# One Trainium2 core, a blocked fp16 matmul with per-row scales: each row tile's output factor is made on ScalarE in place of GpSimd, and the written-out orders are replaced

## The chip, the core and the metric

One core of a Trainium2 chip runs the whole program. The metric is the time of one execution on the device in microseconds (us). Engines are named as the profile names them: PE is TensorE (matmuls), DVE is VectorE, ACT is ScalarE, POOL is GpSimd, SP is SyncE, which issues all DMAs of this kernel. A "step" in this text is four matmuls of 128x128 by 128x512.

## What is computed

```python
def reference(x, w):                      # x: (8, 2048, 2048) f32, w: (2048, 2048) f32
    cs = np.cumsum(x, axis=1)
    diff = cs - np.concatenate([zeros, cs[:, :-1, :]], axis=1)
    return np.matmul(diff, w).astype(np.float32)
```

The difference of a running sum is x again, so the kernel computes x @ w: 16,384 rows (128 row tiles of 128 rows) by 2048 columns.

## The kernel before

**Stages.** The first four row tiles (PLAIN = 4) are multiplied plainly in bf16 while w streams in from HBM: steps `plain.h.r.ko` (column half h, row tile r, block ko of the inner dimension; two matmuls, one for h = 0 and r = 3). Ahead of them stand 30 `warm` matmuls on zeros and eight groups `turn x.q.a` of eight transposes, which turn the first rows on PE (`cast x` on DVE makes them bf16, `turned x` copies them out of PSUM). Each w block is loaded (`w.h.ko`, 512 KB), cast to bf16 on ACT (`cast w`) and searched for its largest magnitude on DVE (`max w`). From those maxima come `uw` and `uinv`, the factors that put w into fp16.

The remaining 124 row tiles go through groups of four, one group to a "period" (period 0 is `group_plain`, periods 1 to 30 are `group`). A group takes the row tiles g, h = g+2, g+1 and h+1, so its 512 rows by 2048 columns are a 2x2 block product done with seven block products in place of eight, and most of those seven are themselves done in seven quarter products. `P1` to `P5` are such inner seven (class `Quarters`, steps `P1.0` to `P1.6`); `S2g T2`, `S2h T2`, `S3g T3`, `S3h T3` are block products in four steps each. DVE makes the sums and differences of the operands: `S1g`, `S3h` and so on (128x1024), `P5.s1` to `P5.s4` (128x512), `in5.Q3` and others (128x2048), and adds results to results in SBUF (`C11g+P2.g.1`, `add_one`, L576) and in PSUM (`P1.middle`, `P1.last`, L517). ACT copies partial sums out of PSUM (`P1.first`, `P1.out2`, `P1.out4`, L568) and takes scaled results out (`keep C11g.0`, `keep_one`, L565).

**The chain of a row tile** (rows of the next group are prepared during this one; the number in a label is the row tile's place, 4 and 6 being the next g and h, 5 and 7 the next g+1 and h+1). `load4.0`, `load4.1`: two halves of a tile into one of four staging slots F, 512 KB each. `weigh4.0`, `weigh4.1` (ACT, L138): sums of magnitudes of each row. `mean4` (DVE, L157), `scale4` (DVE, L159): the row's scale and its reciprocal. `unit4` (L160): the row's mean times `uw`, a 128x1 value, the factor that every result of that row tile is multiplied with, on ACT in `keep` and on DVE in `add`. `narrow4.0`, `narrow4.1` (ACT, L170): the rows times the reciprocal, to fp16. `turn4.0`, `turn4.1` (DMA transposes). In the group's steady order `unit4` is not read before the next group's `keep C11g.0`.

**What sets the order.** `record` collects every operation with a label and an engine; `emit` sorts them by the table `places` (a number for each label and period; the key None holds the order of periods 3 to 28, while 0, 1, 2, 29, 30 and 31 have their own) and issues them so. Each engine runs its operations in that order, one queue for each engine; waits between engines are semaphores that follow from the order. The 512-wide accumulators are eight PSUM banks, and a bank, a staging slot, a half of the operand room of `P5` (`P5.s3` reuses that of `P5.s1`, `P5.s4` that of `P5.s2`) or the buffer `flow` (which `in1.Q4`, `in5.Q3`, `in3.Q1` and others fill in turn) is overwritten only when its readers are done.

Of the kernel before, what the change touches and what calls it, by code (L numbers as in the profile page):

```python
# [10 lines left out]
def kernel(  # L11
# [108 lines left out]
    def role(t):  # L120
        return t - PLAIN - 4 * period[0]
# [26 lines left out]
    def scale_of(t):  # L148
        if t < END:
            m2 = sums_of.pop(t)  # L150
            m = means_at[t % 4]
            s = scales[t] = scales_at[t % 8]
            u = unit[t] = units_at[t % 8]
            record(
                f"mean{role(t)}",
                "dve",
                lambda: nc.vector.tensor_scalar(m, m2[:, :1], m2[:, 1:], TINY, ADD, MAX),  # L157
            )
            record(f"scale{role(t)}", "dve", lambda: nc.vector.reciprocal(s, m))  # L159
            record(f"unit{role(t)}", "pool", lambda: nc.gpsimd.tensor_scalar(u, m, uw, None, MUL))  # L160
# [967 lines left out]
    for g in range(PLAIN + 4, END, 4):  # L1128
# [8 lines left out]
            'first x.0.2': 0, 'first x.1.1': 1, 'first x.0.0': 2, 'first x.1.3': 3,  # L1137
            'first x.0.3': 4, 'first x.0.1': 5, 'first x.1.2': 6, 'first x.1.0': 7, 'w.0.0': 8,
            'zeros': 9, 'ones': 10, 'numbers': 11, 'numbers turned': 12, 'eye': 13, 'eye#2': 14,
            'eye#3': 15, 'eye#4': 16, 'cast x.0.1': 17, 'cast w.0.0': 18, 'warm.0': 19,  # L1140
            'warm.1': 20, 'warm.2': 21, 'warm.3': 22, 'warm.4': 23, 'warm.5': 24, 'warm.6': 25,
            'warm.7': 26, 'warm.8': 27, 'warm.9': 28, 'warm.10': 29, 'warm.11': 30, 'warm.12': 31,
            'warm.13': 32, 'warm.14': 33, 'warm.15': 34, 'warm.16': 35, 'warm.17': 36,
            'warm.18': 37, 'warm.19': 38, 'warm.20': 39, 'warm.21': 40, 'turn x.0.1': 41,
            'warm.22': 43, 'warm.23': 44, 'warm.24': 45, 'warm.25': 46, 'warm.26': 47,
            'warm.27': 48, 'warm.28': 49, 'turned x.0.1': 50, 'cast x.1.0': 51, 'cast x.0.0': 52,
            'turn x.1.0': 53, 'turned x.1.0': 54, 'cast x.1.1': 55, 'warm.29': 56, 'turn x.0.0': 57,
            'turned x.0.0': 58, 'plain.0.1.0': 59, 'plain.0.0.0': 60, 'w.0.1': 61,
            'plain.0.3.0': 62, 'cast w.0.1': 63, 'plain.0.3.1': 64, 'plain.0.2.0': 65,
            'first x.2.3': 66, 'plain.0.0.1': 67, 'w.0.2': 68, 'plain.0.1.1': 69, 'cast w.0.2': 70,  # L1150
            'plain.0.1.2': 71, 'plain.0.0.2': 72, 'plain.0.2.1': 73, 'turn x.1.1': 74, 'w.0.3': 75,
            'cast w.0.3': 76, 'plain.0.0.3': 77, 'w.0.4': 78, 'cast w.0.4': 79, 'plain.0.1.3': 80,
            'plain.0.2.2': 81, 'plain.0.1.4': 82, 'turned x.1.1': 83, 'plain.0.0.4': 85,
            'max w.0.0': 86, 'max w.0.4': 87, 'w.0.5': 88, 'cast w.0.5': 89, 'plain.0.2.3': 90,
            'plain.0.0.5': 91, 'plain.0.1.5': 92, 'plain.0.3.2': 93, 'plain.0.2.4': 94,
            'plain.0.2.5': 95, 'plain.0.3.3': 96, 'plain.0.3.4': 97, 'first x.2.1': 98,
            'first x.2.2': 99, 'first x.2.0': 100, 'w.0.6': 101, 'cast w.0.6': 102, 'w.0.8': 103,
            'w.0.7': 104, 'first x.3.1': 105, 'w.0.9': 106, 'w.0.10': 107, 'cast x.2.0': 108,
            'turn x.2.0': 109, 'turned x.2.0': 110, 'cast x.2.1': 111, 'max w.0.5': 112,
            'max w.0.3': 113, 'max w.0.8': 114, 'max w.0.1': 115, 'max w.0.2': 116,  # L1160
            'max w.0.7': 117, 'first x.3.0': 118, 'cast x.3.0': 119, 'max w.0.10': 120,
            'max w.0.6': 121, 'first x.3.2': 122, 'first x.3.3': 123, 'w.0.11': 124,
            'cast x.3.1': 125, 'cast w.0.7': 127, 'plain.0.0.6': 128, 'plain.0.3.5': 129,
            'plain.0.1.6': 130, 'cast w.0.8': 131, 'plain.0.2.6': 132, 'turn x.2.1': 133,
            'plain.0.3.6': 134, 'plain.0.0.7': 135, 'plain.0.1.7': 136, 'plain.0.1.8': 137,
            'turned x.2.1': 139, 'plain.0.2.7': 140, 'plain.0.0.8': 141, 'plain.0.3.7': 142,
            'plain.0.2.8': 143, 'cast w.0.9': 144, 'plain.0.1.9': 145, 'plain.0.0.9': 146,
            'cast w.0.10': 147, 'turn x.3.0': 148, 'turned x.3.0': 149, 'cast w.0.11': 150,
            'w.0.12': 152, 'w.0.13': 153, 'w.0.14': 154, 'w.0.15': 155, 'w.1.1': 156, 'w.1.0': 157,
            'max w.0.12': 158, 'max w.0.13': 159, 'max w.0.14': 160, 'max w.0.9': 161,  # L1170
            'max w.0.11': 162, 'max w.1.1': 163, 'max w.0.15': 165, 'plain.0.3.8': 166,
            'plain.0.3.9': 167, 'plain.0.0.10': 168, 'plain.0.2.9': 169, 'plain.0.1.10': 170,
            'plain.0.2.10': 171, 'plain.0.3.10': 172, 'plain.0.3.11': 173, 'turn x.3.1': 174,
            'cast w.0.12': 175, 'turned x.3.1': 176, 'cast w.0.13': 178, 'plain.0.0.11': 179,
            'plain.0.1.11': 180, 'plain.0.0.12': 181, 'plain.0.2.11': 182, 'plain.0.1.12': 183,
            'plain.0.2.12': 184, 'cast w.0.14': 185, 'cast w.0.15': 186, 'w.1.7': 187, 'w.1.2': 188,
            'max w.1.7': 190, 'max w.1.0': 191, 'max w.1.2': 192, 'w.1.3': 193, 'w.1.5': 194,
            'max w.1.5': 195, 'w.1.4': 196, 'w.1.6': 197, 'w.1.9': 198, 'w.1.8': 199, 'w.1.11': 200,
            'w.1.12': 201, 'w.1.13': 202, 'max w.1.3': 203, 'max w.1.6': 204, 'max w.1.4': 205,
            'max w.1.9': 206, 'max w.1.8': 207, 'max w.1.11': 210, 'max w.1.12': 211,  # L1180
            'max w.1.13': 212, 'cast w.1.1': 213, 'plain.0.3.12': 214, 'plain.0.3.13': 215,
            'plain.0.1.13': 216, 'plain.0.0.13': 217, 'plain.0.2.13': 218, 'plain.0.3.14': 219,
            'plain.0.1.14': 220, 'plain.0.3.15': 221, 'plain.0.2.14': 222, 'plain.0.1.15': 223,
            'plain.0.2.15': 224, 'plain.0.0.14': 225, 'plain.0.0.15': 226, 'out.0.3.0': 228,
            'cast w.1.0': 229, 'plain.1.3.0': 230, 'plain.1.3.1': 231, 'out.0.1.1': 232,
            'out.0.1.0': 233, 'plain.1.1.0': 234, 'plain.1.1.1': 235, 'out.0.2.1': 236,
            'out.0.2.0': 237, 'cast w.1.2': 238, 'out.0.0.0': 240, 'out.0.0.1': 241,
            'cast w.1.3': 242, 'plain.1.2.0': 243, 'plain.1.2.1': 244, 'plain.1.1.2': 245,
            'plain.1.2.2': 246, 'cast w.1.4': 249, 'cast w.1.5': 251, 'plain.1.0.0': 252,
            'plain.1.0.1': 253, 'plain.1.3.2': 254, 'cast w.1.7': 255, 'cast w.1.6': 256,  # L1190
            'plain.1.0.2': 257, 'plain.1.0.3': 258, 'plain.1.1.3': 259, 'cast w.1.8': 260,
            'cast w.1.9': 262, 'plain.1.0.4': 263, 'plain.1.3.3': 264, 'plain.1.1.4': 265,
            'plain.1.2.3': 266, 'plain.1.1.5': 267, 'plain.1.3.4': 268, 'plain.1.3.5': 269,
            'plain.1.0.5': 270, 'plain.1.2.4': 271, 'plain.1.2.5': 272, 'plain.1.2.6': 273,
            'plain.1.3.6': 274, 'plain.1.2.7': 276, 'plain.1.2.8': 277, 'plain.1.0.6': 278,
            'cast w.1.12': 280, 'cast w.1.11': 281, 'w.1.10': 282, 'cast w.1.10': 284,
            'w.1.14': 285, 'w.1.15': 286, 'plain.1.3.7': 288, 'plain.1.3.8': 289,
            'plain.1.0.7': 290, 'plain.1.0.8': 292, 'plain.1.1.6': 293, 'plain.1.1.7': 294,
            'cast w.1.13': 295, 'plain.1.1.8': 296, 'cast w.1.14': 297, 'plain.1.3.9': 298,
            'plain.1.1.9': 300, 'plain.1.0.9': 301, 'plain.1.0.10': 302, 'cast w.1.15': 304,  # L1200
            'plain.1.0.11': 305, 'plain.1.0.12': 306, 'plain.1.0.13': 308, 'plain.1.1.10': 309,
            'plain.1.0.14': 310, 'plain.1.1.11': 312, 'plain.1.2.9': 314, 'plain.1.0.15': 316,
            'plain.1.3.10': 320, 'plain.1.3.11': 321, 'put out.0.1.1': 324, 'load0.0': 325,
# [244 lines left out]
            'C21g+P4.g.0': 2158, 'put1.0.0': 2163,  # L1448
        },
        31: {  # L1450
            'P4.last': 455, 'C21h+P4.h.1': 456, 'put-1.0.1': 496, 'C21h+P4.h.0': 567,
            'put-1.0.0': 1083,
        },
        None: {
# [75 lines left out]
```

## Time and profile before

| | |
|---|---|
| time before, median of 3 runs | 1452.06 us (1451.21 to 1452.2) |
| the profiled execution: its time, its span | 1451.33 us, 1449.5 us |
| PE busy | 1440.0 us (99%), 6706 matmuls |
| DVE busy | 1339.7 us (92%) |
| ACT busy | 1129.8 us (78%) |
| POOL busy | 43.3 us (3%) |
| granted TensorE clock | 1.00 |
| DMA, HBM | mean 243 GB/s over the span; 90% busy in a steady group |

The span runs from the first to the last instruction of the trace; the time of the same execution is 1.83 us longer. A wait is put down to the engine whose semaphore came last. Matmuls are pipelined: four in a row are drawn 1.03 us long, and the next four start 0.86 us after them.

### The profile page before, as it was taken

The numbers are of one execution on the slowest core, as the hardware profiler recorded it, in microseconds if no ns is written. First come the engines' busy times: TensorE is split into PE (matmuls) and PEld (weight loads), VectorE is DVE, ScalarE is ACT, GpSimd is POOL, SyncE is SP. The second block draws the span as 40 slices with busy tenths as digits, with TensorE's granted clock in tenths as the row PEclk, the third lists the DMA queues.
The fourth block names the chain that finished last, engine by engine and source line by source line (L and its number), as shares of the span: only waits on it lengthen the run. The fifth ranks groups of instructions, "written<-read, shape, count | busy, mean of one in ns | idle before, by whom it ended". The sixth has DMA issues, their size and how long they took to land.

```text
span 1449.5 us, 20480 instructions
## 1 busy us (share of the span) xinstructions
PE 1440.0 (99%) x6706; PEld 653.6 (45%) x6706; DVE 1339.7 (92%) x2457; ACT 1129.8 (78%) x1742; POOL 43.3 (3%) x129
## 2 busy tenths in 40 slices
PE   8999999999999999999999999999999999999998
PEld 4444444444444444444444444444444444444443
DVE  6998899999999999999999999999999999999998
ACT  5987678887778877778877788877788777788773
POOL 0000000000000000000000000000000000000000
PEclk9999999999999999999999999999999999999999
DMA  9999978999888899988898888998889988888973
GB/s 362 375 263 263 245 200 235 237 252 252 232 222 240 238 263 238 235 220 236 242 273 224 227 233 239 252 249 229 227 238 237 265 243 230 216 242 241 273 204 111
DMA packets 343788, 351.60 MB, mean 243 GB/s; under 512 B 270976, under 2 KB 270976, under 8 KB 343680
## 3 DMA queue, kind: packets, MB, share of 16 engines
q1 hardware_dynamic: 343680, 350.29, 88.5%
q8 instruction: 52, 0.85, 0.2%
q14 instruction: 56, 0.46, 0.1%
HBM read 150.99 MB, written 134.22 MB: 197 GB/s over the span
## 4 chain that ended last, share of the span: by engine, by line
PE 98%; DMA 2%; DVE 0%; ACT 0%; SPq 0%; issue 0%; DVEq 0%; ACTq 0%
PE b L551 61%; PE b L529 33%; PE b L302 3%; DMA W<-in_w_dram 1%; DMA W<-in_x_dram 0%; PE b L430 0%; DVE arena L576 0%; SPq L245 0%; ACT arena L287 0%; PE b L260 0%; DVE b L517 0%; ACT arena L565 0%; DVEq L1525 0%; ACTq L287 0%
## 5 line engine op out<-in xcount | busy, mean ns | idle before, releaser
L529 PE MATMUL b<-W,x 128*128 128x512 f16 x2176 | 532.5, 379 | 0.0
L576 DVE SCALAR_TENSOR_TENSOR arena<-b,tiny,arena 128x512 f32<-128x512 f32 x612 | 447.3, 745 | 12.8 <-PE b L529 2.9
L551 PE MATMUL b<-W,arena 128*128 128x512 f16 x1640 | 410.1, 379 | 0.0
L551 PEld LDWEIGHTS <-arena 128*128 128x128 f16 x2700 | 264.1, 98 | 318.6 <-DVE arena L517 0.2
L565 ACT ACTIVATE arena<-b,tiny 128x512 f32<-128x512 f32 x496 | 327.2, 687 | 54.6 <-PE b L529 29.5
L170 ACT ACTIVATE F<-F,tiny 128x1024 f16<-128x1024 f32 x246 | 282.6, 1149 | 61.9 <-DVE tiny L159 58.1
L529 PEld LDWEIGHTS <-x 128*128 128x128 f16 x2176 | 212.9, 98 | 256.7
L551 PE MATMUL b<-W,x 128*128 128x512 f16 x1180 | 289.0, 379 | 0.0
L138 ACT ACTIVATE waste<-F 128x1024 uint8<-128x1024 f32 x246 | 259.5, 1055 | 5.1 <-DMA F<-in_x_dram 3.2
L551 PE MATMUL b<-arena 128*128 128x512 f16 x1060 | 262.7, 379 | 0.0
L568 ACT COPY arena<-b 128x512 f32<-128x512 f32 x294 | 169.7, 577 | 89.4 <-PE b L551 66.4
L517 DVE TENSOR_TENSOR b<-b,arena 128x512 f32<-128x512 f32 x294 | 202.8, 691 | 31.6 <-ACT arena L565 29.6
L551 PEld LDWEIGHTS <-x 128*128 128x128 f16 x1416 | 138.6, 98 | 167.1
L517 DVE TENSOR_TENSOR arena<-W 128x2048 f16<-128x2048 f16 (+1 forms) x155 | 182.0, 1175 | 4.6 <-PE b L551 4.5
L568 ACT COPY b<-b 128x512 f32<-128x512 f32 x147 | 83.9, 571 | 85.1 <-PE b L551 61.6
L517 DVE TENSOR_TENSOR arena<-W,arena 128x512 f16<-128x512 f16 (+1 forms) x157 | 87.8, 563 | 6.7 <-PE b L551 6.6
L517 DVE TENSOR_TENSOR arena<-x,x 128x1024 f16<-128x1024 f16 (+1 forms) x180 | 89.1, 507 | 1.3 <-PE b L551 1.3
L517 DVE TENSOR_TENSOR x<-x,x 128x1024 f16<-128x1024 f16 x124 | 84.7, 684 | 1.0
L160 POOL TENSOR_SCALAR tiny<-tiny 128x1 f32<-128x1 f32 x124 | 42.7, 352 | 1303.2 <-DVE tiny L157 1295.3
L517 DVE TENSOR_TENSOR arena<-arena 128x512 f16<-128x512 f16 x116 | 49.2, 425 | 17.4 <-PE b L551 11.6
L551 PE MATMUL b<-arena,x 128*128 128x512 f16 x236 | 60.2, 379 | 0.0
L302 PE MATMUL b<-arena 128*128 128x512 bf16 x240 | 53.6, 379 | 2.3 <-ACT arena L287 1.4
(44 smaller groups left out, 513.9 us busy)
## 6 DMA issues: line engine op xcount, KB each, us to landing
F<-in_x_dram SPq DMA_DIRECT2D x246, 512.0 KB, 5.9
out_dram<-arena SPq DMA_DIRECT2D x240, 512.0 KB, 4.4
W<-in_w_dram SPq DMA_DIRECT2D x32, 512.0 KB, 9.6
out_dram<-arena SPq DMA_DIRECT2D x32, 256.0 KB, 3.2
W<-in_x_dram SPq DMA_DIRECT2D x16, 256.0 KB, 6.3
x<-F SPq DMA_TRANSPOSE x246, 4.6
arena<-in_x_dram SPq DMA_DIRECT2D x2, 512.0 KB, 5.3
x<-arena SPq DMA_TRANSPOSE x2, 5.4
```

What stands on the lines that cost most here:

```text
L138: lambda: nc.scalar.activation(waste, data, ABS, scale=1.0 / ROW, accum_out=m),
L160: record(f"unit{role(t)}", "pool", lambda: nc.gpsimd.tensor_scalar(u, m, uw, None, MUL))
L170: lambda: nc.scalar.activation(to, data, COPY, scale=s),
L302: said = nc.tensor.matmul(to[n], xP[:, r, ko, :], b[:, ds(n * NB, NB)], start=(ko == 0), stop=(ko == KO - 1),)
L517: record(label, "dve", lambda: nc.vector.tensor_tensor(dst, p, q, op))
L529: said = nc.tensor.matmul(to[n], a[k], b[k][:, n, :], start=(start and k == 0), stop=(k == KH - 1), skip_group_check=True,)
L551: said = nc.tensor.matmul(to, a[k], b[k], start=(start and k == 0), stop=(k == 3), skip_group_check=True)
L565: record(label, "act", lambda: nc.scalar.activation(c, p, COPY, scale=u))
L568: record(label, "act", lambda: nc.scalar.copy(to, p))
L576: label, "dve", lambda: nc.vector.scalar_tensor_tensor(c, p, u, c, MUL, ADD)
```

## The change

```diff
             record(f"scale{role(t)}", "dve", lambda: nc.vector.reciprocal(s, m))
-            record(f"unit{role(t)}", "pool", lambda: nc.gpsimd.tensor_scalar(u, m, uw, None, MUL))
+            record(
+                f"unit{role(t)}",
+                "act",
+                lambda: nc.scalar.activation(u, m, COPY, scale=uw),
+            )
...
     places = {
         0: {
-            'first x.0.2': 0, 'first x.1.1': 1, 'first x.0.0': 2, 'first x.1.3': 3,
+            'first x.0.3': 0, 'first x.0.2': 1, 'first x.1.1': 2, 'first x.1.0': 3, 'w.0.2': 4,
...
```

124 operations of 128x1 leave POOL's queue, whose only other work is `max of all`, and enter ACT's. All tables of `places` get new numbers; the operations themselves, their counts and their sizes are otherwise the same. What the new numbers do to the queues, by stage ("before" and "after" are the two kernels):

Head, loads on SP. Before: x.0.2, x.1.1, x.0.0, x.1.3, x.0.3, x.0.1, x.1.2, x.1.0, w.0.0, w.0.1, x.2.3, w.0.2, w.0.3, w.0.4, w.0.5, x.2.1, x.2.2, x.2.0, w.0.6, w.0.8, w.0.7. After: x.0.3, x.0.2, x.1.1, x.1.0, w.0.2, w.0.0, x.0.1, x.0.0, w.0.1, x.2.0, x.2.3, w.0.3, x.1.2, x.1.3, w.0.5, w.0.4, x.2.1, w.0.6, x.2.2, w.0.7, w.0.9, w.0.8.

Head, DVE. Before: four `eye`, cast x.0.1, turned x.0.1, cast x.1.0, cast x.0.0, cast x.1.1, turned x.0.0. After: cast x.1.0, four `eye`, cast x.0.1, turned x.0.1, max w.0.0, cast x.0.0, turned x.0.0.

Head, PE. Before: 22 warm, turn x.0.1, 7 warm, turn x.1.0, 1 warm, turn x.0.0, then plain.0.1.0; 49 matmuls and three turns stand between there and the first use of w.0.7. After: 19 warm, turn x.0.1, turn x.1.0, 11 warm, turn x.0.0, then plain.0.1.0; 41 matmuls and three turns ahead of the first use of w.0.7.

Steady group, PE, after (51 steps; step 0 is P1.0): P1.0 P2.1 P2.3 P1.2 P2.2 P1.3 P1.4 P1.5 P2.4 P1.6, S2gT2.0.0 P5.0 P2.6 P2.5 S2gT2.1.0 S2gT2.0.1 P5.3 S2gT2.1.1 P5.2 P5.1, S2hT2.1.0 P5.4 P5.5 P3.0 P5.6 S2hT2.0.0 S2hT2.1.1 S2hT2.0.1 P3.1 S3gT3.1.0, P3.2 S3gT3.1.1 P3.3 P3.4 P3.5 P4.0 P3.6 P4.1 S3gT3.0.0 S3gT3.0.1, P4.2 P4.3 S3hT3.0.0 S3hT3.0.1 S3hT3.1.0 P4.4 S3hT3.1.1 P4.5 P4.6, then P1.1 and P2.0 of the next group.

Steady group, ACT from the group's start to weigh6.0. Before: P1.out2, P2.first, narrow7.0, narrow7.1, P2.out2, keep C11g.0, P1.out4, keep C11g.1, P2.out4, keep C11h.0, weigh4.0, weigh4.1, keep C11h.1, P5.first, narrow4.0, narrow4.1, weigh6.0. After: P2.first, P1.first, weigh7.1, P1.out2, narrow7.0, P2.out2, narrow7.1, P1.out4, keep C11g.0, P2.out4, keep C11g.1, **unit5, unit7**, keep C11h.0, weigh4.0, keep C11h.1, weigh4.1, P5.first, narrow4.0, keep C22g.0, keep C12g.0, P5.out2, **unit4**, narrow4.1, weigh6.0. Later in the group **unit6** stands between narrow6.1 and keep C22h.1. unit5 and unit7 are those of the rows weighed in the group before.

Steady group, DVE around P5. Before: C11g+P2.g.1, C11h+P2.h.0, mean4, scale4, P2.last, S1h, P5.s1, P5.s2, C11h+P2.h.1, S3h, P5.s4, P5.s3, P5.middle. After: C11h+P2.h.0, C11g+P2.g.1, mean4, C11h+P2.h.1, scale4, S1h, P5.s1, P5.s2, S3h, S2h, S4h, P5.s4, P5.s3, P5.middle.

End (period 30), the last of PE. Before: P4.4, P4.3, P4.5, P4.6. After: P4.4, S3gT3.1.0, S3gT3.1.1, P4.3, P4.5, P4.6. The last of DVE before: P4.last, C21h+P4.h.1, C21g+P4.g.1, C21g+P4.g.0, C21h+P4.h.0. After: P4.last, C22g+X.1, C21h+P4.h.1, C21g+P4.g.0, C21g+P4.g.1, C21h+P4.h.0.

## The prediction, made before the changed kernel was run

> **What bounds the kernel now.** I read the engines' busy time and slices first, then PE's waits, then the stretch of one steady group (651.04 to 695.07 us, the start of P1.0 to the next).
>
> ```profile
> PE 1440.0 (99%) x6706; PEld 653.6 (45%) x6706; DVE 1339.7 (92%) x2457; ACT 1129.8 (78%) x1742; POOL 43.3 (3%) x129
> ...
> PE   8999999999999999999999999999999999999998
> ...
> PE 98%; DMA 2%; DVE 0%; ACT 0%; SPq 0%; issue 0%; DVEq 0%; ACTq 0%
> ```
>
> ```profile
> PE b L302 <- ACT arena L287: 1.4, 1, 1.4
> PE b L260 <- DVE W L251: 1.2, 1, 1.2
> PE b L338 <- DVE arena L229: 1.2, 1, 1.2
> PE b L302 <- DVE arena L270: 0.8, 1, 0.8
> ```
>
> ```profile
> core 0: us, PE busy (x) PEld busy (x) DVE busy (x) ACT busy (x) POOL busy (x), PEclk, DMA share, GB/s
> 651.04:695.07 44.03, 44.03 (x206) 19.95 (x205) 41.17 (x78) 35.13 (x55) 1.21 (x4) 1.00 0.90 240
> ```
>
> PE waits four times in all, each before 27 us. A busy PE need not be a fast one, so the rate: the chain of waits has "12.95 PE b L551 x60", 0.2158 us a matmul, and a group is 51 steps or 204 matmuls: 204 x 0.2158 = 44.03, exactly its length. From 26.79 us to PE's last end at 1444.6 there is nothing to win without fewer matmuls, and the change leaves 6706. What can move is the head (PE's first real matmul at 12.97, a gap before 26.79), the 4.9 us after PE's end, and, upwards alone, a stall in the groups. A stall in the order of periods 3 to 28 is paid 26 times.
>
> **The unit itself.** Its price on ACT is not in the trace; the nearest rows:
>
> ```profile
> L565 ACT ACTIVATE arena<-b,tiny 128x512 f32<-128x512 f32 x496 | 327.2, 687 | 54.6 <-PE b L529 29.5 <-PE b L551 18.9 <-DMA out_dram<-arena 3.6
> L170 ACT ACTIVATE F<-F,tiny 128x1024 f16<-128x1024 f32 x246 | 282.6, 1149 | 61.9 <-DVE tiny L159 58.1
> ...
> L138 ACT ACTIVATION_READ_ACCUMULATOR waste<-F 128x1 f32 x246 | 47.1, 191 | 0.0
> ...
> L160 POOL TENSOR_SCALAR tiny<-tiny 128x1 f32<-128x1 f32 x124 | 42.7, 352 | 1303.2 <-DVE tiny L157 1295.3 <-DVE W L415 7.9
> ```
>
> The two ACTIVATEs with a scale from memory give (1149 - 687)/512 = 0.90 ns a column and 225 ns at no columns. In the queue such instructions overlap by 0.1 (a `keep` of 0.69 is followed 0.58 to 0.59 later), so the unit takes u = 0.13 to 0.23 of ACT's queue; I take 0.19, the length of the 128x1 row. The far bound is a whole 128x512 row, 0.57; below nothing it can't go. The Trainium skill, "ScalarE: Activation LUTs", section "What ACT_TABLE_LOAD costs", gives about 280 ns plus 0.833 ns a column for an ACTIVATE with one pointer operand and an overlap of some 93 ns; by it u would be 0.19 too, the upper half of what the two rows allow, which speaks against the change. At 1024 columns it gives 1133 ns where the trace has 1149.
>
> ACT has 35.13 us in 44.03; with four units 35.9. That is no bound; its order may be. On POOL nothing stands behind the unit but the next one, so its leaving frees no queue. The operation issues no DMA.
>
> **The steady group.** I set PE's after order on its own clock (step k starts at 0.863k after P1.0 and is drawn 1.03 long) and ask of each step whether its maker is done, with starts and gaps as these rows have them, for P2.4 to P5.4:
>
> ```profile
> 664.27 1.06 ACT L138 ACTIVATE waste<-F 128x1024 uint8<-128x1024 f32 x1
> ...
> 665.45 0.21 DVE L157 TENSOR_SCALAR tiny<-tiny 128x1 f32<-128x1 f32 x1 [0.38 <-ACT waste L138]
> ...
> 667.08 0.89 DVE L517 TENSOR_TENSOR arena<-arena 128x512 f16<-128x512 f16 x2
> ```
>
> Here a mean starts 1.18 after the weigh it needs (and waits for it), and P5.s1 and P5.s2 end at 667.97; P5.2 starts at 668.31, so 0.34 was left. After:
>
> ACT. P2.4 is step 8 and ends at 7.94. P2.out4 7.97, keep C11g.1 8.44 (0.47 after a copy), units from 9.03, keep C11h.0 9.03 + 2u, weigh4.0 +0.59, keep C11h.1 +1.05, weigh4.1 +0.59, mean4 +1.18: 12.44 + 2u, with u = 0.19 12.82.
> DVE. P2.5 is step 13 and ends at 12.25; C11g+P2.g.1 12.28, and DVE is ready for mean4 0.67 later, at 12.95. So the weigh comes first, by 0.13, and 2u is hidden up to 0.51. Then C11h+P2.h.1 13.08, scale4 13.73, S1h 13.80, P5.s1 14.51 (0.71, it needs S1h), P5.s2 14.97 to 15.39; a matmul follows its maker by 0.06 (the cast of 8.14, 0.69 long, and PE at 8.89): 15.45. P5.2 is step 18: 15.54. **0.09 left.**
> On: S3h 15.31, S2h 15.91, S4h 16.62 (needs S2h), P5.s4 17.22, P5.s3 17.56 to 17.99, plus 0.06 18.05; P5.4 is step 21: 18.13. **0.08 left**, where before had 0.24.
> The others have more: P1.5 (P1.middle ends at 5.68, step at 6.04) 0.36, P5.0 0.35, S2gT2.0.0 0.4, P3.5 0.5, P4.2 0.5. unit4 stands ahead of P5.out4, which then starts at 19.36 to 19.93 for P5.6 at 20.72; unit6 ahead of P3.out2, which waits for P3.2 in any case.
> SP: weigh7.0 moves from 45.96 to 41.0. Its load follows put2.1, which follows C12h+Y.0, now at 34.7 and not 36.7; with 5.4 to landing (37.20 to 42.57 before) it is there at 40.6. If late, P2.first behind it waits for 44.5 anyway, so 1.8 more are covered. turn5.1 (issued by 39.5, landed by 45) is 3 us ahead of S1g.
>
> So the groups stay at 44.03. The first two groups, read in the same way, keep 0.25 or more at each step I followed (the tightest is keep C22.0#2 for S4h B22.0.0); a stall there is paid once.
>
> **The head.**
>
> ```profile
> 12.97 4.27 PE L302 MATMUL b<-arena 128*128 128x512 bf16 x18 [0.79 <-DVE arena L270]
> ...
> 24.97 0.38 PE L302 MATMUL b<-arena 128*128 128x512 bf16 x1
> 26.79 3.91 PE L302 MATMUL b<-arena 128*128 128x512 bf16 x17 [1.44 <-ACT arena L287]
> ```
>
> The four `eye` operations were done before any x had landed; now they wait behind cast x.1.0, whose x is the fourth load (7.38): cast 7.48, eye 8.10 to 9.25, cast x.0.1 9.20 (8.14 before), turn 9.95, turned 10.60, max w.0.0 11.21, cast x.0.0 12.34, turn x.0.0 13.22 (its cast is done at 13.03, the 11 warm matmuls at 13.2), turned to 14.57: first real matmul at 14.62, 1.65 later. But the gap before 26.79 is a wait for w.0.7, and loads land one behind another, 0.66 us for 256 KB and 1.28 for 512 KB. In after it is the 20th load, with 7 MB landed like before's 20th, at 24.33 in the trace (25.61 before, the 21st). Cast 24.43 to 25.47, PE at 25.52; PE itself would be there at 25.0. Eight fewer matmuls are done by then, 1.73: 25.52 + 1.73 = 27.25 against 26.79, **+0.46**. Later w blocks arrive 0.05 or more ahead (w.0.13 the closest). Range 0 to +1.7, the latter if nothing of the later start is absorbed.
>
> **The end.**
>
> ```profile
> 1443.40 2.73 DVE L576 SCALAR_TENSOR_TENSOR arena<-b,tiny,arena 128x512 f32<-128x512 f32 x4
> ...
> 1443.58 1.03 PE L551 MATMUL b<-W,x 128*128 128x512 f16 x4
> ```
>
> Before, four adds run from 1443.40 to 1446.13, 2.55 after P4.6 starts, since P4.last had waited for P4.out4 until 1442.67. With two steps moved behind P4.4, out4 comes 1.73 earlier: counted from P4.6, P4.last -2.64, C22g+X.1 -1.53 (S3gT3.1.1 ends at -1.56), C21h -0.86, C21g.0 -0.19, C21g.1 +0.48, C21h.0 +1.15 to 1.90: **-0.65**. The put behind it is the same.
>
> Sum: 1451.33 + 0.46 - 0.65 = 1451.1 for an execution like the profiled one. That one lies 0.73 below the median of 1452.06; so 1451.9.
>
> **Rivals.**
> *Slower: the two units lengthen ACT's chain to P5.2.* It decides once 2u is over 0.51, plus the 0.09: u over 0.30; or if the DVE chain behind C11g+P2.g.1 is 0.1 longer than its gaps of before. For it: 0.09 and 0.08 are no more than my reading error over six instructions, and a wait of ACT on another semaphore has no row. Against: u by rows is 0.23 at most, and POOL's units held DVE up in before (scale5 comes 0.45 after mean5, scale4 only 0.25 after mean4). Price: 26 x 0.1 = 2.6 us for each 0.1; with u = 0.57 26 x (1.14 - 0.60) = 14 us. 1454 to 1466.
> *Slower once: the head keeps its 1.65 and one of the new orders of periods 0 to 2, 29 and 30 stalls 1 to 3 us.* 1453 to 1456. Against: w.0.7's landing takes part of it back, and the steps I followed had cover.
> *Faster: DVE, free of POOL's neighbour, runs ahead.* [...] But PE waits for DVE nowhere in a group, so 0.2 x 4 a group buys margin, not time. Over 0.2% would need 2.9 us out of a head gap of 1.6 and the end: 1449.
>
> **Chances and range.** A difference of 0.2%, 2.9 us, is about what a measurement can tell from no change here. Forecast (the groups keep 44.03, head and end cancel, 1450.5 to 1454) 0.62; ACT's or DVE's chain stalls P5.2 or P5.4 0.24, nearly all over 2.9 us; one-off stalls over 2.9 us 0.10; faster by over 2.9 us 0.04. So faster 0.04, same 0.62, slower 0.34. The range runs from 1450.5 (head 0, end -0.65, and the 0.85 by which the fastest run before lies below the median) to 1457.5, a stall of 0.2 a group.
>
> **What would show it.** Right: the group still 44.03 long, PE's waits all before 27 us, ACT's busy time some 25 us up and POOL's under 1, the first real matmul near 14.6, the last DVE add 1.9 after P4.6's start. Wrong: PE waits on DVE L517 or ACT in 26 equal pieces, a 128x1 ACTIVATE over 0.3 us, or a mean that waits for its weigh ahead of P5.

## The result, and the profile after

The changed kernel takes 1456.2 us (median of 8 runs, 1454.72 to 1457.54), the kernel before 1451.67 (8 runs beside it, 1451.02 to 1452.2): a ratio of 1.003, 95% interval 1.0021 to 1.0039. The prediction gave 1451.9 and a chance of 0.62 to a time within 2.9 us (0.2%) of the one before: the kernel is slower by 4.5 us, more than that, though inside the range of 1450.5 to 1457.5.

The profiled execution took 1457.06 us, 0.9 over that median and 5.73 more than the profiled execution before; its span is 1455.3. Here are the profile page's line of busy times, PE's row of slices and the chain of waits by engine:

```profile
PE 1443.8 (99%) x6700; PEld 652.1 (45%) x6706; DVE 1341.3 (92%) x2457; ACT 1132.9 (78%) x1866; POOL 0.5 (0%) x5
...
PE   8999999999999999999999999999999999999998
...
PE 97%; DVE 1%; DMA 1%; issue 0%; ACT 0%; SPq 0%; DVEq 0%; ACTq 0%
```

Nothing here tells where 5.7 us are: PE is as full as before. (6 of its 6706 matmul records are missing.) So I set the k-th weight load of PE in the one trace against the k-th in the other and asked how much later it starts. That delay is 3.84 us at the 1000th load and had been so since the 400th, so it arises in the head, the stretch of the start; it grows by 0.06 in each of the 26 groups of periods 3 to 28, to 5.37; it grows by 0.66 in period 30, to 6.03; and VectorE's last add ends 5.34 later than before. **3.84 head + 1.53 groups + 0.66 period 30 - 0.69 end = 5.34**; the last 0.4 of the 5.73 lies behind that add.

PE's waits in full, and the weight loads' largest wait (line, what it waited for, total us, times, longest):

```profile
PE b L264 <- DVE W L255: 3.6, 1, 3.6
PE b L342 <- DVE arena L233: 1.2, 1, 1.2
PE b L306 <- DVE arena L274: 0.8, 1, 0.8
PE b L264 <- DVE arena L274: 0.8, 1, 0.8
```

```profile
PEld L555 <- DVE arena L521: 17.2, 54, 0.6
```

By its own list PE still waits nowhere after 20 us. A stall of 0.06 is too short for that list; it shows in the loads, which wait 54 times for a sum of VectorE, about twice in each group, and in the length of the group (P1.0 to the next P1.0, period 12):

```profile
613.96:658.05 44.09, 44.09 (x205) 19.87 (x204) 41.21 (x77) 35.11 (x59) 0.00 (x0) 1.00 0.86 238
```

**The head.** PE's timeline from the start to the first real matmuls, and the granted clock (PEclk, third column from the end) in three stretches of it:

```profile
1.17 5.66 PE L342 MATMUL b<-arena 128*128 128x512 bf16 x19 [1.17 <-DVE arena L233]
10.44 0.71 PE L264 MATMUL b<-waste,W 128*128 128x128 bf16 x8 [3.61 <-DVE W L255]
11.94 1.01 PE L264 MATMUL b<-waste,W 128*128 128x128 bf16 x8 [0.78 <-DVE arena L274]
12.74 4.90 PE L342 MATMUL b<-arena 128*128 128x512 bf16 x11
17.43 0.72 PE L264 MATMUL b<-waste,W 128*128 128x128 bf16 x8
18.94 3.41 PE L306 MATMUL b<-arena 128*128 128x512 bf16 x14 [0.79 <-DVE arena L274]
```

```profile
8.00:10.00 2.00, 0.00 (x0) 0.00 (x0) 1.92 (x6) 0.74 (x1) 0.00 (x0) 1.00 0.99 392
10.00:13.00 3.00, 1.78 (x17) 1.51 (x18) 2.19 (x4) 1.34 (x2) 0.00 (x0) 0.64 1.05 413
13.00:17.00 4.00, 4.00 (x10) 1.32 (x9) 0.61 (x2) 2.28 (x3) 0.00 (x0) 0.50 1.05 403
```

PE stands still for 3.61 us before turn x.0.1, and just after it is given work again, at 10.83, its clock drops to a half, until 17.66. The 11 dummies between turn x.1.0 and turn x.0.0 start 0.427 us apart instead of 0.216: 4.69 us from the first of them to the turn, not 2.37. The first real matmul, that is the first of the `plain` steps, comes at 18.94.

**The group around P5.** VectorE's rows there, and PE's P5.4, whose operand P5.s3 is the second of the pair at 631.33:

```profile
629.27 0.68 DVE L521 TENSOR_TENSOR x<-x,x 128x1024 f16<-128x1024 f16 x1
629.99 0.69 DVE L521 TENSOR_TENSOR x<-arena,x 128x1024 f16<-128x1024 f16 x1
630.72 0.69 DVE L521 TENSOR_TENSOR x<-x,x 128x1024 f16<-128x1024 f16 x1
631.33 0.76 DVE L521 TENSOR_TENSOR arena<-arena 128x512 f16<-128x512 f16 x2
```

```profile
632.14 1.04 PE L555 MATMUL b<-arena 128*128 128x512 f16 x4
```

S3h, S2h, S4h start 0.72 and 0.73 apart; P5.s3 ends at 632.09 and P5.4 follows at 632.14, 18.18 after P1.0, where its step is due at 18.13.

**The unit and the end.** The group of the 124 units, ACT's row, and the last rows of VectorE and of PE:

```profile
L163 ACT ACTIVATE tiny<-tiny 128x1 f32<-128x1 f32 x124 | 33.2, 289 | 0.6 <-DVE tiny L157 0.6
```

```profile
1448.08 3.39 DVE L580 SCALAR_TENSOR_TENSOR arena<-b,tiny,arena 128x512 f32<-128x512 f32 x5 [0.32 <-PE b L533]
```

```profile
1449.61 1.03 PE L555 MATMUL b<-W,x 128*128 128x512 f16 x4
```

A unit is drawn 0.29 long, and unit7 starts 0.19 after unit5 (9.22 and 9.04 into the group): that 0.19 is what it takes of the queue. The last add ends at 1451.47, 1.86 after P4.6 starts.

### The profile page after: what moved, and what is told of

The parts are those of the page before. It is cut to its first block, busy times and chain, and to the rows that moved or that the text cites. A ratio compares the mean times of both kernels' runs of the same rounds, so it can differ in the third digit from the quotient of the medians.

```text
span 1455.3 us, 20086 instructions
## 1 busy us (share of the span) xinstructions
PE 1443.8 (99%) x6700; PEld 652.1 (45%) x6706; DVE 1341.3 (92%) x2457; ACT 1132.9 (78%) x1866; POOL 0.5 (0%) x5
## 4 chain that ended last, share of the span: by engine, by line
PE 97%; DVE 1%; DMA 1%; issue 0%; ACT 0%; SPq 0%; DVEq 0%; ACTq 0%
PE b L555 60%; PE b L533 33%; PE b L306 4%; DMA F<-in_x_dram 1%; DVE arena L580 0%; DMA W<-in_x_dram 0%; PE b L342 0%; PE b L264 0%; PE b L434 0%; DVE arena L521 0%; ACT F L174 0%; DVE arena L274 0%; SPq L249 0%; DVE b L521 0%; DVE waste L224 0%
## 5 line engine op out<-in xcount | busy, mean ns | idle before, releaser
L580 DVE SCALAR_TENSOR_TENSOR arena<-b,tiny,arena 128x512 f32<-128x512 f32 x612 | 442.4, 744 | 13.5 <-PE b L555 5.1
L569 ACT ACTIVATE arena<-b,tiny 128x512 f32<-128x512 f32 x496 | 329.0, 686 | 27.9 <-PE b L533 13.0
L555 PE MATMUL b<-arena 128*128 128x512 f16 x1060 | 267.1, 379 | 0.0
L521 DVE TENSOR_TENSOR arena<-arena,x 128x512 f16<-128x512 f16 x118 | 49.7, 421 | 1.8
L521 DVE TENSOR_TENSOR arena<-x,arena 128x512 f16<-128x512 f16 x118 | 49.5, 420 | 0.6 <-PE b L555 0.6
```

Of the source, the lines that this page charges most:

```text
L521: record(label, "dve", lambda: nc.vector.tensor_tensor(dst, p, q, op))
L555: said = nc.tensor.matmul(to, a[k], b[k], start=(start and k == 0), stop=(k == 3), skip_group_check=True)
L569: record(label, "act", lambda: nc.scalar.activation(c, p, COPY, scale=u))
L580: label, "dve", lambda: nc.vector.scalar_tensor_tensor(c, p, u, c, MUL, ADD)
```

## The experiments

Two theories after the comparison. **A**: the unit on ACT costs nothing; the new orders cost everything, and of the head's 3.84 the lowered clock is the greater part (theory **C**: idling PE lowers the clock that it is granted a few us later). **B**: the units on ACT push something late. The table has PE's delay against the trace before, at its 1000th weight load ("head"; in e4 this holds stalls of periods 0 to 2) and from there to the end of period 28 ("groups"). Times are medians of several executions, the delays are those of the one profiled execution of each kernel.

| kernel | median us | before beside it | ratio (95%) | head | groups |
|---|---|---|---|---|---|
| after | 1456.2 | 1451.67 | 1.003 (1.0021 to 1.0039) | 3.84 | 1.53 |
| e5, unit back on POOL | 1456.45 | 1451.33 | 1.0031 (1.0019 to 1.0042) | 3.86 | 1.53 |
| e4, before with the unit on ACT | 1452.3 | 1451.65 | 1.0006 (0.9997 to 1.0015) | 1.64 | 0 |
| e12, after with nine more dummies | 1453.55 | 1451.12 | 1.0019 (1.001 to 1.0028) | 0.67 | 1.53 |
| e1, after, all dummies ahead | 1454.66 | 1451.65 | 1.0021 (1.0012 to 1.0031) | 2.72 | 1.52 |
| e2, after, eyes first | 1453.26 | 1451.65 | 1.0011 (1.0002 to 1.002) | 0.81 | 1.54 |
| e9, after without 11 dummies | 1454.93 | 1451.33 | 1.0023 (1.0014 to 1.0032) | 2.27 | 1.93 |
| e3, after, P5.s3 first | 1454.08 | 1451.65 | 1.0018 (1.0009 to 1.0027) | 2.30 | 0 |
| e7, e2 and e3 together | 1451.79 | 1451.33 | 1.0003 (0.9994 to 1.0012) | -0.09 | 0 |
| e10, e7 with PE idling | 1451.38 | 1451.29 | 1.0001 (0.9992 to 1.001) | -0.08 | 0 |
| e6, before with PE idling | 1451.84 | 1451.33 | 1.0003 (0.9995 to 1.0012) | 0.17 | 0 |
| e8, before, late units, an end of my own (another result) | 1453.8 | 1451.29 | 1.0016 (1.0007 to 1.0025) | -0.44 | 0 |
| e11, before, late units, after's end | 1451.67 | 1451.12 | 1.0003 (0.9994 to 1.0012) | -0.40 | 0 |

### Is it the unit, or the orders?

**e5** takes the changed kernel and gives the unit back to POOL.

```diff
-            record(
-                f"unit{role(t)}",
-                "act",
-                lambda: nc.scalar.activation(u, m, COPY, scale=uw),
-            )
+            record(f"unit{role(t)}", "pool", lambda: nc.gpsimd.tensor_scalar(u, m, uw, None, MUL))
```

> The changed kernel with its new orders kept, and the units computed on GpSimd again. Theory A (the unit itself costs nothing on the path; the new orders of the head, the steady groups and period 30 cost everything): no gain, the time of the changed kernel, 1454.7 to 1457.5 us, groups of 44.09 us, the first real matmul at 18 to 19 us. Theory B (ScalarE's 124 units push something late): the time falls to 1453 us or less and the groups to 44.03 us.

As theory A: 1456.45, head, groups and first real matmul (18.96) as in the changed kernel. The orders cost it all, and theory B falls for this kernel.

**e4** does the reverse: the kernel before with all its numbers, and only the unit's engine changed.

> The before kernel, with the unit alone moved to ACT and every place as before. Theory U (124 operations of 0.29 us on ACT cost time): groups longer than 44.03, time up by 1 us or more. The other theories (the orders cost it, not the engine): groups of 44.03, the time of before, 1451.7, within 0.5.

Neither reading held as written: its groups stay at 44.03 and the median rises by 0.65 alone, but PE loses 1.64 us in one-off stalls of periods 0 to 2. The largest three are 0.4 at 87 us, 0.5 from 148 to 153 and 0.7 at 194. ACT's timeline at the first of them, before and in e4, and PE in e4:

```profile
83.28 1.25 ACT L565 ACTIVATE arena<-b,tiny 128x512 f32<-128x512 f32 x2
```

```profile
83.37 0.65 ACT L163 ACTIVATE tiny<-tiny 128x1 f32<-128x1 f32 x3
84.45 0.29 ACT L163 ACTIVATE tiny<-tiny 128x1 f32<-128x1 f32 x1 [0.43 <-DVE tiny L157]
84.65 1.25 ACT L569 ACTIVATE arena<-b,tiny 128x512 f32<-128x512 f32 x2
```

```profile
86.76 3.63 PE L533 MATMUL b<-W,arena 128*128 128x512 f16 x16 [0.21 <-DVE arena L521]
```

Four units stand ahead of keep C11g.0, the last of them waits 0.43 for its mean, and the keep starts at 84.65 instead of 83.28. On POOL that wait held up nobody. So a unit on ACT is not free everywhere: it costs where ACT is behind. The times alone (+0.65, interval through zero) could not have shown it.

**e8** and **e11** test that. Both are the kernel before with ACT making the units from tile 16 on and POOL those ahead of it; both also change the end.

```diff
-            record(f"unit{role(t)}", "pool", lambda: nc.gpsimd.tensor_scalar(u, m, uw, None, MUL))
+            on_act = t - PLAIN >= 16
+            record(
+                f"unit{role(t)}",
+                "act" if on_act else "pool",
+                lambda: nc.scalar.activation(u, m, COPY, scale=uw)
+                if on_act
+                else nc.gpsimd.tensor_scalar(u, m, uw, None, MUL),
+            )
```

The end of e8, an order of my own:

```diff
+    places[30].update({"P4.4": 1999.5, "P4.out4": 2012, "C21g+P4.g.0": 2094})
+    places[31]["P4.last"] = 412.5
```

The end of e11, the changed kernel's numbers for the 53 labels from P4.s1 on and for period 31:

```diff
+    places[30].update({
+        "P4.s1": 2038, "P3.last": 2052, "P4.s2": 2058, "in4.Q1": 2041, "P3.5": 2044,
...
+    })
+    places[31].update({
+        "P4.last": 502, "C21h+P4.h.1": 504, "put-1.0.1": 507, "C21h+P4.h.0": 638,
+        "put-1.0.0": 1083,
+    })
```

> The kernel before in its own orders, with two edits: from the third group of steady steps on (tiles 16 and later) ScalarE makes the units, GpSimd those of the tiles before; and in the end P4.4 is put ahead of S3h T3.1.1, with P4.out4 and P4.last that follow it. Theory D (a unit on ScalarE costs only where ScalarE has a backlog, in the first three periods): the one-off stalls of e4 (0.4 at 87 us, 0.5 from 148 to 153, 0.7 at 194) are gone and the groups stay at 44.03 us. The end: the four last adds on VectorE follow one another from 0.5 us earlier, so 0.3 to 0.6 less: 1451.0 us or so, within what can be told from no change, best seen in the end of VectorE's last add (1446.13 us before, 1445.5 to 1445.8 here). Rival (units on ScalarE cost wherever they stand): stalls of about 0.2 us for each unit in the groups from the fourth on, 1452.3 or more.

> The kernel before in its own head and groups, with ScalarE's units from tile 16 on, and with the changed kernel's order for the end (the part of period 30 from P4.s1 on, and period 31). If the changed kernel's end is worth 0.65 to 0.69 by itself and late units cost nothing: groups of 44.03 us, no one-off stall, VectorE's last add 0.6 to 0.7 earlier than before's at the same start of the last period, so some 1450.7 us; that is 0.04% and cannot be told from no change in the times, only in the trace. If the end's gain belongs to the changed kernel's groups (their other phase), the last add comes as late as before or later: 1451.3 or more.

In both PE's delay is constant from the 300th load to the end of period 28 (-0.44 and -0.40; the negative sign is an earlier landing of w.0.7 in those executions): 108 units on ACT, no stall, as theory D. The two ends differ. In e8 my edit put P4.4 ahead of in4.Q3, the difference that makes one of its operands, so the last group multiplies what lay in the buffer `flow` before, and the result is another one; VectorE then stood still until P4.4 had read that buffer (2.51 us ahead of in4.Q3): the last add ends at 1447.40, the time is 1453.8 us, and of the end nothing can be read here. In e11, with the changed kernel's order:

```profile
1441.78 3.38 DVE L583 SCALAR_TENSOR_TENSOR arena<-b,tiny,arena 128x512 f32<-128x512 f32 x5 [0.33 <-PE b L536]
```

The last add ends at 1445.16, 0.97 earlier than before, of which 0.40 is the head, 0.13 was lost in period 30 and 0.70 is the end. So the end's gain belongs to its order and travels with it. The median, 1451.67 against 1451.12, does not show it: the gain is 0.05%, and these times do not resolve that.

### The head: is it the clock?

**e12** fills the idle stretch. Nine dummies more, put after warm.18; the rest of the changed kernel stays, its late turns too.

```diff
-    WARM = 30
+    WARM = 39
...
+    for i in range(30, 39):
+        places[0][f"warm.{i}"] = 33 + (i - 29) / 100
```

> The changed kernel with nine more dummy matmuls ahead of turn x.0.1, where TensorE idles 3.6 us; all else as in it, the wait for bank 7 and the later turns included. Theory C (the idle lowers the clock): the clock stays at 1.00, the eleven dummies after turn x.1.0 take 2.4 us instead of 4.7, the first real matmul comes at 16.5 to 17 us instead of 18.94, and the time falls by about 2, to 1453.8 to 1454.6. What then remains of the head is 1.5 to 2 us against before, from the later turns and the bank. Rival (the clock falls for another reason, or the head's loss is all in the later turns): as the changed kernel, 1455.5 to 1456.5.

PE's timeline and the same stretches of clock:

```profile
1.17 9.17 PE L342 MATMUL b<-arena 128*128 128x512 bf16 x28 [1.17 <-DVE arena L233]
...
12.01 2.54 PE L342 MATMUL b<-arena 128*128 128x512 bf16 x10
...
15.78 3.63 PE L306 MATMUL b<-arena 128*128 128x512 bf16 x16 [0.79 <-DVE arena L274]
```

```profile
10.00:13.00 3.00, 2.22 (x23) 1.47 (x22) 2.26 (x4) 1.38 (x2) 0.00 (x0) 1.00 1.04 410
13.00:17.00 4.00, 3.16 (x21) 1.62 (x20) 0.93 (x2) 2.22 (x3) 0.00 (x0) 1.00 1.05 404
```

More work on PE, and the kernel is faster: 1453.55, which is 2.4 over the kernel before beside it and not 4.5. The clock stays at 1.00, the first real matmul comes at 15.78, and the head's delay falls from 3.84 to 0.67. So 3.17 of the 3.84 is the idle stretch and the clock behind it; theory C holds here. Nearly all of that is the clock and not the standing still: turn x.0.1 starts at 10.18 here, only 0.26 earlier than in the changed kernel. What remains is less than the 1.5 to 2 expected, since some of the later start is absorbed by landings after all.

**e1** goes the other way about it: all 30 dummies run ahead of the turns.

```diff
+    for i in range(19, 30):
+        places[0][f"warm.{i}"] = 33 + (i - 18) / 100
```

> The after kernel with one thing changed in its head: the 11 warm matmuls that stood behind turn x.1.0 now stand ahead of turn x.0.1, so PE has work while the first x is on its way (its idle time before turn x.0.1 shrinks from 3.6 us to about 1.2) and none between turn x.1.0 and turn x.0.0. Loads, DVE and ACT keep their orders. Theory C (the idle PE is given a lower clock, and the head's loss is that): no stretch of the head under a clock of 0.9, first real matmul at about 15.0 in place of 18.9, time 3 to 4 us below the after kernel, near 1452.5. Theory L (the eye step stands behind cast x.1.0, so everything on DVE is late whatever the clock): DVE is as late as in after, no more than 1 us is won. Theory U (the units on ACT cost the time): nothing is won.

```profile
10.00:13.00 3.00, 1.23 (x16) 0.94 (x16) 2.29 (x4) 1.34 (x2) 0.00 (x0) 1.00 1.04 411
13.00:17.00 4.00, 2.52 (x13) 1.19 (x15) 1.11 (x2) 2.25 (x3) 0.00 (x0) 0.63 1.05 403
```

Missed: the first real matmul does come at 14.88, but the time is 1454.66 and the clock falls all the same. The longest wait ahead of it is now 1.23, but four follow one another (1.23, 0.78, 1.12, 0.79) with only turns between; from 10 to 13 us PE works 1.23 of 3. The clock falls later, to 0.63 from 13 to 17 us and 0.50 from 17 to 20, and there the real matmuls run: 14 of them take 5.75 us. It is not one long wait that counts, but how little PE does in a stretch.

**e9** leaves the same 11 dummies out altogether.

```diff
-    for i in range(WARM):
+    for i in range(19):
         warm(i)
```

> The changed kernel without its dummy matmuls warm.19 to warm.29, the eleven that run at a low clock between turn x.1.0 and turn x.0.0. If those eleven are the head's loss (they sit on the path, and 11 of them take 4.69 us): turn x.0.0 follows its cast at 13.7 us, the first real matmul comes at about 15.4 and the time falls to 1453. If the loss is the low clock, whoever runs in it: TensorE idles even more, the first real matmul comes at about 15.4 all the same but the real matmuls run in the slow stretch, and the time stays at 1454.5 to 1457.

```profile
14.76 6.24 PE L306 MATMUL b<-arena 128*128 128x512 bf16 x16 [0.79 <-DVE arena L274]
```

```profile
13.00:17.00 4.00, 3.14 (x14) 1.50 (x15) 1.14 (x3) 2.36 (x3) 0.00 (x0) 0.53 1.04 400
17.00:20.00 3.00, 3.00 (x9) 1.07 (x8) 1.65 (x3) 0.15 (x1) 0.00 (x0) 0.50 1.03 402
```

The second reading: the first real matmul is 4.2 earlier than in the changed kernel, and 16 real ones then take 6.24 us instead of 3.63. The dummies are not the loss; whoever runs in the slow stretch pays. (Of e9's 1.93 in the groups, 0.4 is one stall at 937 us that the other runs do not have; its cause was not followed.)

**e2** mends the cause of the idling: the four `eye` operations, which wait for nothing, ahead of cast x.1.0, and that cast behind turned x.0.1, as in the kernel before.

```diff
+    places[0].update({"eye": 11.2, "eye#2": 11.3, "eye#3": 11.4, "eye#4": 11.5, "cast x.1.0": 40.5})
```

> The after kernel with DVE's head order mended: the four eye operations and cast x.0.1, turned x.0.1 stand ahead of cast x.1.0; PE's order is after's. turn x.0.1 then starts when the 19 warm matmuls end (6.9), PE's longest idle time is some 1.5 to 2 us. Theory C: full clock or nearly, first real matmul at about 14, time 3.5 to 4.5 us below the after kernel, near 1452. Theory L: the same. The two differ in e1, not here. Theory U: nothing is won.

The clock is 1.00 in every stretch from 7 us on, the first real matmul comes at 14.43, the head's delay 0.81 with a wait of 1.15 for w.0.7 in it. The eleven executions lie within 0.56 us; those of the changed kernel spread over 2.8, those of e1 too. The median, 1453.26, is 2.9 below the changed kernel and not 3.5 to 4.5: the groups' 1.54 is still in it, which the expectation had not set apart.

**e6** and **e10** try the same on kernels whose head is sound. Both leave eleven of the dummies out ahead of turn x.0.1, e6 in the kernel before, e10 in e7. This is e6's edit; in e10 the range is `8 <= i < 19`.

```diff
     for i in range(WARM):
-        warm(i)
+        if not 11 <= i < 22:
+            warm(i)
```

> The kernel before without its dummy matmuls warm.11 to warm.21, so that TensorE idles some 4 us longer before turn x.0.1; nothing that is stored depends on them. Theory C (a stretch in which TensorE is mostly idle lowers the clock that it is granted a few us later): the clock in the slices from 10 to 20 us falls to 0.5 to 0.8 and the time rises by 1.5 to 4 us, to 1453.2 to 1455.7. Rival (dummy matmuls are off the path, and the changed kernel's slow dummies had another reason): 1451.7, clock 1.00 throughout.

> The mended kernel e7 without its dummy matmuls warm.8 to warm.18, so that TensorE idles some 3 us before turn x.0.1; nothing else differs. Theory C (3 us of idle in a stretch lower the granted clock for some us): the clock falls to 0.5 to 0.8 between 8 and 14 us, the first real matmul comes 1.0 to 2.0 us later than in e7 (14.38 us); what reaches the groups is that less the 0.47 us that TensorE waits at 25 us in e7 anyway, so 0.5 to 1.5 us. Rival (the dummies have no effect on the clock): all as in e7, first real matmul at 14.4, 1451.8 us.

PE idles 2.85 us in e6; the clock:

```profile
8.00:10.00 2.00, 1.10 (x10) 0.78 (x11) 1.08 (x2) 0.00 (x0) 0.00 (x0) 0.83 1.07 416
10.00:13.00 3.00, 3.00 (x16) 1.40 (x14) 2.11 (x4) 1.04 (x1) 0.00 (x0) 0.54 1.04 414
```

The clock fell as theory C says, to 0.54 in e6 and to 0.69 and 0.64 from 8 to 13 us in e10, yet the time did not rise: half of each expectation failed. In e6 the first real matmul came 1.64 later than before (14.61), and the wait for w.0.7 took all but 0.17 of it back. In e10 the eleven dummies after the turn took 4.22 instead of 2.54 but were done just as turn x.0.0's cast was (first real matmul 14.24, against 14.38 in e7). In these runs a lowered clock cost only what reached past the next wait. In the changed kernel the first real matmul came so late that w.0.7, landed by 23.6, was no longer waited for, and nothing gave the loss back.

### The groups

**e3** swaps P5.s3 and P5.s4 in the steady order, since P5.4 reads P5.s3.

```diff
+    own = places[None]
+    own["P5.s3"], own["P5.s4"] = own["P5.s4"], own["P5.s3"]
```

> The after kernel with P5.s3 and P5.s4 exchanged on DVE in periods 3 to 28. In after P5.s3 ends 18.12 us after P1.0 and P5.4 was due at 18.13; ahead of P5.s4 it ends at 17.88. If the 0.06 us by which each of these 26 groups is longer is the wait for P5.s3, the groups are 44.03 long again and 1.5 us are won (1454.7); if it is ACT's chain with the two units, the groups stay at 44.09 and nothing is won. The head keeps its loss in either case.

The delay of PE is 2.30 at the 1000th load and 2.30 at the 6400th, the group is 44.03, and the loads' waits halve:

```profile
PEld L555 <- DVE arena L521: 7.4, 28, 0.6
```

That the head also differs here (2.30, not 3.84) is not the edit's doing, which lies in the steady order alone: executions of one kernel differ in how long the clock is low. Of e3's eleven, the three with a mean clock of 1.000 took 1451.83 to 1452.17 us and the three with 0.997 took 1455.19 to 1455.62. So e3's median, 2.1 under the changed kernel where 1.5 was expected, holds some of that spread. In the changed kernel the order is rougher: the three at 0.997 took 1457.06 to 1457.54, the four at 0.998 1454.72 to 1456.85, the one at 1.000 1454.94.

**e7** puts e2's and e3's edits together.

> The changed kernel with both mendings together: the identity tiles and cast of e2, and the swap of P5.s3 and P5.s4 of e3. If the parts add: head +0.8 against before, steady groups 44.03 (0), period 30 +0.1 to +0.7, end -0.7: in all +0.2 to +0.8, so 1451.9 to 1452.5 us, and the narrow spread of e2. If instead the groups' delay was a consequence of the head's, or the reverse, the sum fails by more than 0.7.

1451.79: head -0.09 (expected 0.8; the landing again, with a wait of 0.47 instead of 1.15), groups 0, period 30 +0.59, end -0.69, sum -0.19 in the trace. That is under the +0.2 to +0.8 expected, because the head cost 0.9 less than expected. The losses of the head and of the groups are separate and add up; that of period 30 stays.

**Period 30** was not mended. In the changed kernel weigh7.1 stands ahead of P1.first on ACT and waits there for the last load ("1.65 <-DMA F<-in_x_dram" before it at 1407.71); P1.2, P1.4 and P5.1 slip by 0.16, 0.31 and 0.19. The loss goes with that wait: it is 0.66, 0.69 and 0.59 where the wait is 1.65, 1.52 and 1.66 (after, e3, e7), 0.13 where it is 1.14 (e2), 0.02 at 0.96 (e1), and nothing at 0.59 or less (e5, e12, e9, e10). No run takes weigh7.1 out of that place, so this cause is read from the traces and not tested.

No kernel tried beats the one before by an amount that the times can tell; e10 and e11, with the shortest spans (1449.2 and 1449.0 against 1449.5), are the nearest.

## Why the prediction failed, point by point

- **The unit: right, with some luck.** u was 0.19, taken as the drawn length of another 128x1 row; the unit is drawn 0.29 long, and its 0.19 of the queue is that less an overlap of 0.1. The bounds of 0.13 to 0.23 held. It is hidden in the steady groups (e5, e11), so the rival "ACT's chain to P5.2" is refuted: mean4 starts 12.96 into the group (12.95 worked out), P5.s2 ends at 15.40 (15.39), and P5.2 starts on time at 15.54. The prediction did not ask where ACT is behind; in e4's periods 0 to 2 it was, and the changed kernel's new order for them had cover, as forecast.
- **The head: the step that failed.** It read "turn x.0.0 13.22 (its cast is done at 13.03, the 11 warm matmuls at 13.2)", and so took each dummy at 0.216 us. They measured 0.427. The first real matmul came 4.32 later than forecast (18.94, not 14.62), of which 3.16 is gone in e12 (15.78), where the clock stays up; and the head cost 3.84, not 0.46. The sum itself held PE's wait: 19 dummies are done at 6.83 in the trace, the turn was forecast at 9.95, so PE had 3 us of nothing. I asked what that wait does to the first matmul, not what it does to the clock, and read "granted clock 1.00" of before as a property of the chip and not of an order that kept PE busy. The Trainium skill, "TensorE: Matmul & The Clock Gate", section "What's actually happening", says that an idle window of some 3.4 us, free-running, halves the clock, and a busy one restores it; the 0.50 here agrees, and so do the low stretches of 3.41 us or twice that; the 0.427 us agrees with the 426.7 ns that the section "Wait — 56ns, not 53.3ns?" of the same page of the Trainium skill gives for the lowered clock; and "free-running" fits e3's executions. The section "Why this matters for your kernels" of that page of the Trainium skill warns of gaps over some 3 us; here 2.85 (e6) and 2.71 (e3) were enough, and so were waits of 1.23, 0.78, 1.12 and 0.79 with little between them.
- **Two smaller errors in the head.** The working missed that turn x.1.0 waits for bank 7 until turned x.0.1 has emptied it ("0.78 <-DVE arena L274"), and that the fourth load lands at 7.80, not 7.38. Without the clock they would have mattered little: in e12, which keeps the wait for bank 7 and lands that load at 7.50, the first real matmul is 1.16 later than forecast, and the head is +0.67 against the +0.46 forecast, inside the range of 0 to 1.7.
- **The groups: the margin was named, a term of 0.12 mis-sized.** "P5.4 is step 21: 18.13. 0.08 left" used 0.60 from S3h to S2h, the interval that S2h had before behind P5.middle (671.18 after 670.58), with which it shares nothing. Behind S3h it measured 0.72: S2h writes over A11h, which S3h reads, and starts only after S3h has ended. S4h behind it came 0.73 after S2h, not 0.71: 0.08 - 0.14 is the -0.06 seen. P5.2's 0.09 held. The first rival priced such a stall right (26 x its length) and had VectorE's gaps as its second cause, after ACT's chain; it was that second cause, at P5.4 and not at P5.2, and smaller than the 0.1 it reckoned with.
- **The range held by luck.** Its upper end stands for a stall of 0.2 in each group; the groups lost 0.06, and most of the rest came from the head.
- **The rival "slower once"** asked for a stall of 1 to 3 us in period 0 to 2, 29 or 30, or the head. Most of the loss is of this kind (3.84 + 0.66), by a mechanism that it did not name, and 0.10 was too low a chance for it.
- **The end: right.** -0.65 forecast, -0.69 measured, and 1.86 from P4.6 to the last add (1.90 forecast).
- **ACT's busy time** was to rise by some 25 us and rose by 3.1, though the units' own rows sum to 33.2. Two runs take it apart: e4, the units in the old orders, has 1151.3, which is 21.5 more than before; e5, the new orders without units, has 1111.5, which is 18.3 less. So the price was about right, and the new orders take most of it off again: ACT waits less ahead of its keeps (27.9 us instead of 54.6), more of its rows start before the row ahead has ended (1355 in e5, 1170 before, by 0.1 each), and time in which two overlap is counted once.
- **The "faster" rival**: POOL out of VectorE's way brought PE nothing. e5, with POOL back, is the same to 0.3 us. The rows do not show that POOL held VectorE up, either: the 0.45 from mean5 to scale5 (687.68 and 688.13 before) has another instruction in it, P4.s3 at 687.80, which the old order puts between the two; scale4 stands right behind mean4.

## What to carry to other kernels

An order that lets TensorE idle early can be paid twice: once in the later start (0.67 us here, e12), once in the clock of the few us behind it (3.17). So when a reordering moves a matmul later, sum PE's idle time over a few us, price what runs next at half rate, and ask whether a later wait takes the loss back, as in e6. Dummies that fill the gap cost less than the gap did (e12: nine more matmuls, 2.1 us less). Margins under 0.1 us in a step repeated 26 times have to be summed with the interval of a dependent pair, not of a free one.

Whether a small operation moved to an idle-looking engine is free was decided here by where that engine is behind, in periods 0 to 2 (e4), and not by its share of busy time.

## What the runs showed of the hardware

- The granted clock fell to 0.5 after PE had done little for about 3 us: with single waits of 3.61 (after), 2.71 (e3) and 2.85 us (e6), and with split ones (e1, e9, and e10 with 0.91 and 2.03). It stayed at 1.00 in the heads whose longest wait behind the first dummies was 1.48 (e4), 1.44 (before), 1.39 (e2, e7) or 0.78 us (e12).
- In these traces it changed in steps of 3.41 us, counted from the first record of the clock, which lies at 4.01 us in the changed kernel and between 3.81 and 7.18 in the other heads. It fell at the end of a step in which PE was busy for 0.39 (after), 0.46 (e5), 0.56 (e6), 1.07 (e10), 1.10 (e3), 1.41 (e9) or 1.50 us (e1), and not at the end of one with 1.60 (e9), 1.98 (e4), 2.02 (e2, e7) or more. It rose at the end of a step in which PE was busy throughout (e3, e6, e10: low for 3.41), and not after one with 2.41 to 2.63 (e1, after, e5, e9: low for 6.83). Most of the work in the steps ahead of a fall was turns, so it stays open whether the busy time decides or the kind of work.
- Ahead of that first record the views print 1.00, but the dummies start 0.43 apart there and 0.22 from it on (before: until 4.51; e2: until 7.1). So 1.00 says nothing of the first 4 to 7 us of a trace.
- At a granted 0.50, 128x512 bf16 matmuls start 0.427 us apart instead of 0.216; VectorE's casts of 128x1024 keep their 0.68 to 0.69.
- On VectorE a sum of 128x1024 in fp16 starts 0.60 after a sum that it has nothing to do with (632.60 after 632.00 and 1383.81 after 1383.21 in the changed kernel), that is before the first has ended; it starts 0.72 after one of its own shape whose operand it writes over, 0.03 after that one's end.
